# Turning token tiles and p by DMA instead of TensorE, ahead of attention and of the per-layer embedding

## The chip, the cores and the metric

The kernel runs on one core of one Trainium2 chip. The metric is the device time of one execution in microseconds; the kernel before takes 1997.2 us (median of 3 runs, 1996.89 to 1997.23).

## The reference

Two layers of a block are computed for 512 tokens of width 1024, in float32. A layer has four parts, each followed by a residual and a layer norm: a gated FFN (width 2816), a token mixer (stick-breaking attention, a chunked gated delta rule and a short convolution, called attention here), a second FFN, and the per-layer embedding.

```python
def reference(x, p, ln_g, ln_b, ffn_w_in, ...):
    for i in range(DEPTH):                                     # DEPTH = 2
        x = layer_norm(ALPHA * x + 0.5 * swiglu(x, ffn_w_in[i, 0], ffn_w_out[i, 0]), ln_g[i, 0], ln_b[i, 0])
        mix = token_mix(x, mix_w_in[i], ..., mix_w_out[i])
        x = layer_norm(ALPHA * x + mix, ln_g[i, 1], ln_b[i, 1])
        x = layer_norm(ALPHA * x + 0.5 * swiglu(x, ffn_w_in[i, 1], ffn_w_out[i, 1]), ln_g[i, 2], ln_b[i, 2])
        ple = jax.nn.sigmoid(x @ ple_w_gate[i] + ple_b_gate[i]) * (p[i] @ ple_w_proj[i])
        x = layer_norm(ALPHA * x + ple, ln_g[i, 3], ln_b[i, 3])
    return x
```

x is 512 x 1024, p is 512 x 256 for each layer, `ple_w_gate` 1024 x 1024, `ple_w_proj` 256 x 1024.

## The kernel before

The 512 tokens are four tiles (t = 0 to 3) of 128 tokens, the partitions of a core. x lies in SBUF twice: `x_tok`, tokens on the partitions, in float32, for residuals and norms; and `xT`, features on the partitions, for the matrix products, as two float16 parts, hi and lo, with lo the remainder after hi. Every product is three float16 matmuls (`mm3`, L278, L281, L282: hi by hi, hi by lo, lo by hi).

Weights come from memory in float32 by SyncE's DMA queue into one of three `raw` buffers (`load_rows`, 1 MB each). `split_part` makes the two halves: ScalarE copies raw, scaled, to hi (L141), VectorE subtracts (L142); a weight buffer has two such splits of 128x1024. A raw buffer is free for the next load when VectorE has made the second split from it.

The stages of a layer run one after the other: FFN, attention, FFN, embedding. An FFN works in four groups of hidden rows; at the end of each, `out_proj` multiplies the group's activations, up to four buffers `hT` of 4 KB a partition, by the output weights, tile by tile into the bank `po` (36 matmuls a tile in the last group), and VectorE adds to `x_tok` (L525). In the last group `norm_tile` follows each tile: statistics (L185, L187, L189), and four operations over 128x512 (L193, L197). `layer_norm` then puts the tile on the list `pending`.

`flush` turns what is pending: `to_T` does eight 128x128 float32 transposes on TensorE (L232) into two PSUM banks; ScalarE copies each bank to hi (L237), VectorE subtracts to lo (L238). It is called one tile later, so that TensorE has the next tile's products to do while the norm runs; the fourth tile's comes in the following stage.

The embedding (`ple`) loads four gate weights and the projection, one ring (`w1`) of five buffers of 8 KB beside a small pool for the bias `bg`, the norm constants and `pT`. For each tile it does the gate product (`pgate`, 48 matmuls), the projection of p (`pp`), sigmoid, product, residual and norm. p is loaded as `pr` and turned by 16 transposes on TensorE after the first tile's gate (L572), with L576 and L577 as its copies to hi and lo.

No order between the engines is written out: the tile framework's scheduler sets each engine's order when the program is built, by priorities and by its own cost model, and adds semaphore waits where a buffer or a value needs them. Pools that close give their space to the next ones, so the buffers of one stage lie where those of the stage before lay, and the first writes there wait for their last readers. Where the order on one engine is fixed by hand, `self.after(later, earlier)` ties two instructions without a semaphore. SyncE issues almost all transfers, in the order of its queue; an instruction there that waits holds all behind it.

The lines that the change touches, with what calls them, are these.

## Time and profile before

| | |
|---|---|
| median of 3 runs | 1997.2 us (1996.89 to 1997.23) |
| the profiled execution | 1997.55 us, span 1995.8 us, granted clock 0.998 |
| TensorE busy | 1950.1 us, 98% of the span |
| VectorE busy | 1522.4 us, 76% |
| ScalarE busy | 868.8 us, 44% |
| transposes of x on TensorE (L232) | 256, 36.1 us busy |
| transposes of p on TensorE (L572) | 16, 2.4 us busy |

Busy times of TensorE are sums of single durations that overlap in its pipeline; how long a batch holds the engine is read from the starts in order of time. In such rows the first number is the start in us from the span's beginning, the second the busy time of the merged rows, then engine, line, operation, output and inputs, and in brackets the idle time before it and what ended it. Stage by stage, the first layer's first FFN ends at 341.1 us, its second at 944.1 us.

### The profile page before, as it was taken

How to read it: one execution, taken by the hardware profiler on the slowest of the kernel's cores; microseconds unless marked ns; L12 is line 12 of the kernel's file. 1: busy time of each engine (PE TensorE's matmuls, PEld its weight loads, DVE VectorE, ACT ScalarE, POOL GpSimd, SP SyncE). 2: the span in 40 equal slices, each digit the busy share in tenths (PEclk: the TensorE clock that was granted, in tenths of full speed). 3: DMA queues.
4: the chain of work that ended last, by engine and by line, in shares of the span. 5: the costliest groups of instructions: out<-in, count | busy, mean ns of one | idle time of the engine just before them, and what ended most of it. 6: DMA issues, size and time to landing. Idle time of an engine off the chain costs nothing.

```text
span 1995.8 us, 33106 instructions
## 1 busy us (share of the span) xinstructions
PE 1950.1 (98%) x14058; PEld 1273.0 (64%) x14058; DVE 1522.4 (76%) x2347; ACT 868.8 (44%) x1294; POOL 69.9 (4%) x92
## 2 busy tenths in 40 slices
PE   7999999999999999999999999999999999999998
PEld 6677686545546677686467685854455466776853
DVE  8996866775679895859897877577756897967586
ACT  6454352454335453444264453424643364443431
POOL 1000000100000000000000000002000000000000
PEclk9999999999999999999999999999999999999999
DMA  8543320422162433334224343212222534333221
GB/s 239 184 126 103 89 86 1 130 56 64 65 196 79 148 106 106 106 120 146 94 85 127 106 124 88 65 55 78 53 86 82 173 96 138 106 106 85 96 74 43
DMA packets 245359, 205.15 MB, mean 103 GB/s; under 512 B 20846, under 2 KB 225500, under 8 KB 245212
## 3 DMA queue, kind: packets, MB, share of 16 engines
q1 hardware_dynamic: 245212, 203.05, 33.0%
q8 instruction: 110, 1.80, 0.4%
q14 instruction: 37, 0.30, 0.0%
HBM read 200.14 MB, written 2.88 MB: 102 GB/s over the span
## 4 chain that ended last, share of the span: by engine, by line
PE 73%; DVE 17%; ACT 6%; issue 2%; DMA 1%; POOL 0%; SPq 0%; DVEq 0%; ACTq 0%
PE po L282 7%; PE po L278 7%; PE po L281 7%; PE pA L278 6%; PE pA L281 6%; PE pA L282 6%; DVE wq L142 4%; DVE w L142 3%; PE pB L282 3%; PE pB L281 3%; PE pB L278 3%; ACT wq L141 2%; DVE f L492 1%; PE pC L281 1%; PE pC L282 1%
## 5 line engine op out<-in xcount | busy, mean ns | idle before, releaser
L142 DVE SCALAR_TENSOR_TENSOR wq<-f,wq 128x1024 f16<-128x1024 f32 (+1 forms) x240 | 335.2, 1399 | 18.4 <-ACT wq L141 15.3
L141 ACT ACTIVATE wq<-f 128x1024 f16<-128x1024 f32 (+1 forms) x240 | 279.4, 1191 | 126.5 <-PE pB L282 84.4
L141 ACT ACTIVATE w<-raw 128x1024 f16<-128x1024 f32 (+1 forms) x196 | 192.6, 1030 | 257.1 <-PE po L282 224.0
L278 PE MATMUL pA<-xS,wq 128*128 128x256 f16 x960 | 261.5, 272 | 7.9 <-ACT sg L447 3.9
L278 PE MATMUL po<-w,hT 128*128 128x512 f16 x704 | 266.9, 379 | 1.9 <-ACT hT L310 1.3
L282 PE MATMUL po<-w,hT 128*128 128x512 f16 x704 | 264.8, 379 | 2.7 <-DVE hT L311 2.7
L281 PE MATMUL po<-w,hT 128*128 128x512 f16 x704 | 266.8, 379 | 0.0
L282 PE MATMUL pA<-xS,wq 128*128 128x256 f16 x960 | 261.6, 273 | 0.0
L281 PE MATMUL pA<-xS,wq 128*128 128x256 f16 x960 | 261.6, 272 | 0.0
L142 DVE SCALAR_TENSOR_TENSOR w<-raw,w 128x1024 f16<-128x1024 f32 (+1 forms) x196 | 229.7, 1197 | 33.0 <-ACT w L141 33.0
L281 PEld LDWEIGHTS <-wq 128*128 128x128 f16 x2240 | 219.1, 98 | 44.8 <-issue 14.4
L492 DVE TENSOR_TENSOR f<-f 128x512 f32<-128x512 f32 x320 | 220.2, 690 | 27.2 <-DMA f<-in_ffn_w_in 22.1
L278 PEld LDWEIGHTS <-wq 128*128 128x128 f16 x2240 | 219.1, 98 | 29.9
L282 PEld LDWEIGHTS <-wq 128*128 128x128 f16 x2240 | 219.1, 98 | 27.1
L525 DVE SCALAR_TENSOR_TENSOR x_tok<-po,x_tok 128x512 f32<-128x512 f32 x144 | 97.5, 687 | 82.9 <-PE po L282 82.9
L282 PEld LDWEIGHTS <-hT 128*128 128x128 f16 x704 | 68.0, 98 | 86.2 <-DVE hT L311 6.5
L428 DVE TENSOR_TENSOR sg<-pB,sg 128x256 f32<-128x256 f32 x80 | 33.9, 423 | 115.6 <-PE pB L282 115.6
L278 PEld LDWEIGHTS <-hT 128*128 128x128 f16 x704 | 68.9, 98 | 79.7 <-ACT hT L310 3.4
L447 ACT ACTIVATE sg<-pA 128x256 f32<-128x256 f32 x80 | 30.6, 383 | 203.6 <-PE pA L282 203.6
L281 PEld LDWEIGHTS <-hT 128*128 128x128 f16 x704 | 68.9, 98 | 77.3 <-issue 1.5
L281 PEld LDWEIGHTS <-w 128*128 128x128 f16 x640 | 62.5, 98 | 61.3 <-issue 13.4
L282 PEld LDWEIGHTS <-w 128*128 128x128 f16 x640 | 62.5, 98 | 60.3 <-issue 5.4
(290 smaller groups left out, 3825.2 us busy)
## 6 DMA issues: line engine op xcount, KB each, us to landing
f<-in_ffn_w_in SPq DMA_DIRECT2D x160, 512.0 KB, 5.0
raw<-in_ffn_w_out SPq DMA_DIRECT2D x44, 1024.0 KB, 5.6
raw<-in_mix_w_in SPq DMA_DIRECT2D x28, 1024.0 KB, 5.5
raw<-in_mix_w_out SPq DMA_DIRECT2D x8, 1024.0 KB, 4.8
raw<-in_ple_w_gate SPq DMA_DIRECT2D x8, 1024.0 KB, 5.9
raw<-in_ffn_w_in SPq DMA_DIRECT2D x6, 1024.0 KB, 5.8
ln_gb<-in_ln_g SPq DMA_DIRECT2D x8, 512.0 KB, 3.9
ln_gb<-in_ln_b SPq DMA_DIRECT2D x8, 512.0 KB, 4.8
```

The source lines that it names most:

```text
L141: self.nc.scalar.activation(hi, raw, AF.Copy, scale=WS),
L142: self.nc.vector.scalar_tensor_tensor(lo, raw, WS, hi, op0=ALU.mult, op1=ALU.subtract),
L278: begun = nc.tensor.matmul(ps, a[0], b[0], start=first, stop=False, **k)
L281: nc.tensor.matmul(ps, a[0], b[1], start=False, stop=False, **k)
L282: return nc.tensor.matmul(ps, a[1], b[0], start=False, stop=last, **k)
L428: nc.vector.tensor_tensor(half(old.sg, 1), old.B, half(old.sg, 1), op=ALU.add)
L447: nc.scalar.activation(half(u.sg, 1), u.A, AF.Copy)
L492: total = nc.vector.tensor_tensor(f[:, to], f[:, a], f[:, b], op=ALU.add)
L525: self.nc.vector.scalar_tensor_tensor(xs, po[h], scale, xs, op0=ALU.mult, op1=ALU.add)
```

## The change

Attention and the embedding now get most of their turned tiles by transposing DMA. `pair_T` copies a tile in float16 into one buffer `turn` (ScalarE, 128x1024) and the remainder into a second (VectorE), and SyncE issues two `dma_start_transpose`, hi and lo, straight into `xT`. `turn`, called at the end of `layer_norm`, chooses by what stage follows: ahead of attention, tiles 0 to 2 are turned by DMA at once and tile 3 stays on TensorE by way of `pending`; ahead of an FFN all stay on TensorE; ahead of the embedding all four are kept on the list `turns` and done in `ple`: tiles 0 to 2 in SyncE's queue behind the projection's load, then bias and norm constants, then tile 3. p is loaded and turned the same way in the last group of the FFN before (`load_early`), as are the rows of constants for attention loaded; they have pools of their own, `tmp4` and `early`. The embedding's pool no longer holds `pT`.

```diff
@@ -41,12 +42,15 @@
         self.rawp = pool("rawp", bufs=3)
         self.w2 = pool("w2", bufs=4)
         self.tmp = pool("tmp", bufs=6)
+        self.tmp4 = pool("tmp4", bufs=2)
+        self.early = pool("early", bufs=1)
         self.small = pool("small", bufs=4)
         self.dram = pool("dram", bufs=2, space=bass.MemoryType.DRAM)
         self.psa = pool("psa", bufs=2, space=PSUM)
         self.psb = pool("psb", bufs=3, space=PSUM)
         self.psc = pool("psc", bufs=3, space=PSUM)
         self.pending, self.block_sums, self.put, self.behind = [], [], 0, None
+        self.turns = []
         self.constants()
 
     def bank(self, name, shape=(P, 512)):
@@ -171,9 +175,10 @@
         gb = pool.tile([P, 2, D], F32, name="ln_gb", tag=tag or "ln_gb", **k)
         g, b = gb[:, 0], gb[:, 1]
         dma = self.nc.sync.dma_start(g, self.ins["ln_g"][i, j : j + 1, :].to_broadcast([P, D]))
-        self.nc.sync.dma_start(b, self.ins["ln_b"][i, j : j + 1, :].to_broadcast([P, D]))
+        self.consts = self.nc.sync.dma_start(b, self.ins["ln_b"][i, j : j + 1, :].to_broadcast([P, D]))
         if after is not None:
             self.after(dma, after)
+            self.after(self.consts, after)
         return g, b
 
     def layer_norm(self, t, y, gb, last=False):
@@ -202,7 +207,7 @@
                     self.out[t * P : (t + 1) * P, h * 512 : (h + 1) * 512], yh
                 )
         if not last:
-            self.pending.append((self.xT, t, y, self.next_sums))
+            self.turn(self.xT, t, y)
 
     def norm_tile(self, t, gb, last):
 
@@ -259,6 +264,58 @@
             held.append(step)
         else:
             step()
+
+    def pair_T(self, out, pieces, wide=False):
+
+
+        nc = self.nc
+        hi, lo = (self.t2("turn", (P, D), F16) for _ in range(2))
+        if wide:
+            pieces, n = [pieces], D
+        else:
+            n = 512
+        for c, y in enumerate(pieces):
+            h, l = (v[:, c * n : (c + 1) * n] for v in (hi, lo))
+            if len(y.shape) == 3:
+                h, l = (v.rearrange("p (a b) -> p a b", b=y.shape[2]) for v in (h, l))
+            nc.scalar.activation(h, y, AF.Copy)
+            nc.vector.tensor_tensor(l, y, h, op=ALU.subtract)
+        return [nc.sync.dma_start_transpose(out(q), v) for q, v in enumerate((hi, lo))]
+
+    def turn(self, xT, t, y):
+
+
+        kind = self.following[2]
+        if kind == "p" and kind in KINDS:
+            self.turns.append((xT, t, y))
+        elif kind not in KINDS or t == NT - 1:
+            self.pending.append((xT, t, y, kind not in KINDS and kind == "f"))
+        else:
+            self.turn_now(xT, t, y)
+
+    def turn_now(self, xT, t, y, behind=None):
+        dmas = self.pair_T(lambda q: xT[:, q, :, t * P : (t + 1) * P], y, wide=True)
+        for dma in dmas if behind is not None else []:
+            self.after(dma, behind)
+        return dmas[1]
+
+    def load_early(self):
+
+        nc, ins = self.nc, self.ins
+        i, j, kind = self.following
+        if kind == "m":
+            rows = self.rows = self.early.tile([55, P], F32, name="rows", tag="rows")
+            nc.sync.dma_start(rows[0:48], ins["gdn_conv_w"][i].rearrange("t (c p) -> (t c) p", p=P))
+            nc.sync.dma_start(rows[48:54], ins["sc_conv_w"][i].rearrange("t (c p) -> (t c) p", p=P))
+            nc.sync.dma_start(rows[54:55], ins["gdn_norm_w"][i : i + 1, :])
+        if kind == "p":
+            pr = self.tmp4.tile([P, NT, 256], F32, name="pr", tag="ts")
+            nc.sync.dma_start(pr, ins["p"][i, 0].rearrange("(t p) e -> p t e", p=P))
+            pT = self.pT = self.tmp4.tile([P, 2, 2, S], F16, name="pT", tag="ts")
+            self.pair_T(
+                lambda q: pT[:, q].rearrange("p c (t k) -> p (c t) k", k=P),
+                [pr[:, :, c * P : (c + 1) * P] for c in range(2)],
+            )
 
     def put_sums(self, xS):
 
@@ -457,6 +514,8 @@
                 wo = weights((m1 - m0) // 2)
                 if gi == len(groups) - 1:
                     gb = self.ln_consts(i, j, self.w2, tag="w")
+                    if not last:
+                        self.load_early()
                 for t in range(NT):
                     self.out_proj(
                         t, lambda q, m: hT[(m0 + m) // 2][:, q, m % 2], wo, m1 - m0,
@@ -530,17 +589,17 @@
         self.xT = self.act.tile([P, 2, KD, S], F16, name="xT", tag="xT", bufs=2)
         with self.tc.tile_pool(name="ple", bufs=1, reuse_waits="tile") as pool, \
                 self.tc.tile_pool(name="w1", bufs=5, reuse_waits="tile") as self.w1:
-            pr = [self.t2("pr", (P, 2, 256)) for _ in range(2)]
-            for h in range(2):
-                nc.sync.dma_start(
-                    pr[h], ins["p"][i, 0, 256 * h : 256 * h + 256].rearrange("(t p) e -> p t e", p=P)
-                )
             wg = [self.load_rows(ins["ple_w_gate"][i], k, self.w1) for k in range(0, KD, 2)]
             wp = self.load_rows(ins["ple_w_proj"][i], 0, self.w1)
+
+            for args in self.turns[:-1]:
+                dma = self.turn_now(*args, behind=self.loaded)
             bg = pool.tile([P, D], F32, name="bg")
-            self.after(nc.sync.dma_start(bg, ins["ple_b_gate"][i : i + 1, :].to_broadcast([P, D])), self.loaded)
-            gb = self.ln_consts(i, j, pool)
-            pT = pool.tile([P, 2, 2, S], F16, name="pT")
+            self.after(nc.sync.dma_start(bg, ins["ple_b_gate"][i : i + 1, :].to_broadcast([P, D])), dma)
+            gb = self.ln_consts(i, j, pool, after=dma)
+            self.turn_now(*self.turns[-1], behind=self.consts)
+            self.turns = []
+            pT = self.pT
 
             def gift(t, h, behind=None):
                 pp = self.bank2("pp")
@@ -565,19 +624,6 @@
                         )
                     if last and t == NT - 1:
                         pps[h], done = gift(t, h, end)
-                if t == 0:
-                    for c in range(2):
-                        ps = self.bank2("ps_p", (P, NT, P))
-                        for tt in range(NT):
-                            nc.tensor.transpose(
-                                ps[:, tt], pr[tt // 2][:, tt % 2, c * P : (c + 1) * P], self.ident
-                            )
-                        hi = pT[:, 0, c].rearrange("p (t q) -> p t q", t=NT)
-                        nc.scalar.activation(hi, ps, AF.Copy)
-                        nc.vector.tensor_tensor(
-                            pT[:, 1, c].rearrange("p (t q) -> p t q", t=NT), ps, hi,
-                            op=ALU.subtract,
-                        )
                 self.flush()
                 for h in range(2):
                     hs = slice(h * 512, (h + 1) * 512)
@@ -629,10 +675,7 @@
         OFF_Q, OFF_K, OFF_V, OFF_Z, OFF_AB, OFF_SC = 768, 1280, 1792, 2304, 2816, 2824
 
-        rows = self.t2("rows", (55, P))
-        nc.sync.dma_start(rows[0:48], ins["gdn_conv_w"][i].rearrange("t (c p) -> (t c) p", p=P))
-        nc.sync.dma_start(rows[48:54], ins["sc_conv_w"][i].rearrange("t (c p) -> (t c) p", p=P))
-        nc.sync.dma_start(rows[54:55], ins["gdn_norm_w"][i : i + 1, :])
+        rows = self.rows
         hd = sm.tile([P, 2, 2], F32, name="hd", bufs=1)
         for e in range(2):
             for n, name in enumerate(("gdn_a_log", "gdn_dt_bias")):
@@ -1215,7 +1258,7 @@
     k.load_x()
     for (i, j, s), following in zip(n, n[1:] + [None]):
         last = following is None
-        k.next_sums = not last and following[2] == "f"
+        k.following = following
         if s == "f":
             k.ffn(i, 0 if j == 0 else 1, j, last)
         elif s == "m":
```

ScalarE ahead of the first layer's embedding, before (w<-raw are the splits of gate and projection weights; hT<-sg the FFN's last activations; xT<-ps_t the copies of turned tiles):

```order
L141 ACTIVATE w<-raw 128x1024 [waits DMAHW7_49,PE_49]
L310 ACTIVATE hT<-sg 128x512 [waits DVE_49,Activation_49]
L141 ACTIVATE w<-raw 128x1024
L141 ACTIVATE w<-raw 128x1024 [waits DMAHW0_49]
L141 ACTIVATE w<-raw 128x1024
L141 ACTIVATE w<-raw 128x1024 [waits DMAHW1_49]
L141 ACTIVATE w<-raw 128x1024
L141 ACTIVATE w<-raw 128x1024 [waits DMAHW2_49]
L141 ACTIVATE w<-raw 128x1024
L237 ACTIVATE xT<-ps_t 128x4x128 [waits PE_49] x4
L141 ACTIVATE w<-raw 128x1024 [waits DMAHW3_49,PE_49]
L141 ACTIVATE w<-raw 128x1024
```

The same place after (line numbers are those of the changed kernel: L145 is the split, L281 the copies to be turned, L367 the activations):

```order
L281 ACTIVATE turn<-x_tok 128x1024 [waits DVE_49]
L281 ACTIVATE turn<-x_tok 128x1024 [waits DMAHW1_49,DVE_49]
L281 ACTIVATE turn<-x_tok 128x1024 [waits DVE_49]
L145 ACTIVATE w<-raw 128x1024 [waits PE_49]
L145 ACTIVATE w<-raw 128x1024 x3
L145 ACTIVATE w<-raw 128x1024 [waits DMAHW2_49]
L145 ACTIVATE w<-raw 128x1024
L145 ACTIVATE w<-raw 128x1024 [waits DMAHW4_49]
L145 ACTIVATE w<-raw 128x1024
L145 ACTIVATE w<-raw 128x1024 [waits DMAHW5_49]
L145 ACTIVATE w<-raw 128x1024
L281 ACTIVATE turn<-x_tok 128x1024 [waits DMAHW6_49,DVE_49,Activation_49]
```

All splits of the gate's weights now stand behind the copies of tiles 0 to 2, and the first of them waits for TensorE. In the built program that wait is for the sixth matmul from the end of the FFN's last output product. The first gate buffer begins at byte 151424 of a partition, and so does the last of the four `hT` buffers, which that matmul reads; before, the embedding's pool held 4 KB more below the ring.

SyncE's queue at the embedding, before (raw are weights, bg and ln_gb the constants):

```order
L535 DMA pr<-in_p 128x2x256 [waits DMAHW7_49,DVE_49]
L535 DMA pr<-in_p 128x2x256 [waits DMAHW0_49,DVE_49]
L161 DMA raw<-in_ple_w_gate 128x2x1024 [waits DVE_49]
L161 DMA raw<-in_ple_w_proj 128x2x1024 [waits DVE_49]
L150 DMA raw<-in_ffn_w_in 128x8x256 [waits DMAHW3_49,DVE_49]
L150 DMA raw<-in_ffn_w_in 128x8x256 [waits DMAHW1_49,DMAHW4_49,DVE_49,Activation_49]
L161 DMA raw<-in_ffn_w_out 128x2x1024 [waits DMAHW2_49,DMAHW5_49,DVE_49,Activation_49]
L541 DMA bg<-in_ple_b_gate 128x1024 [waits DMAHW6_49,PE_49]
L173 DMA ln_gb<-in_ln_g 128x1024 [waits DMAHW7_49,PE_49]
L174 DMA ln_gb<-in_ln_b 128x1024 [waits DMAHW0_49]
```

And after:

```order
L165 DMA raw<-in_ple_w_proj 128x2x1024 [waits DMAHW5_49,DVE_49]
L283 DMA_TRANSPOSE xT<-turn 128x8x128 [waits DMAHW6_49,PE_49]
L283 DMA_TRANSPOSE xT<-turn 128x8x128 [waits DMAHW7_49]
L283 DMA_TRANSPOSE xT<-turn 128x8x128 [waits DMAHW0_49]
L283 DMA_TRANSPOSE xT<-turn 128x8x128 [waits DMAHW1_49]
L283 DMA_TRANSPOSE xT<-turn 128x8x128 [waits DMAHW2_49]
L283 DMA_TRANSPOSE xT<-turn 128x8x128 [waits DMAHW3_49]
L598 DMA bg<-in_ple_b_gate 128x1024 [waits DMAHW4_49,PE_49]
L177 DMA ln_gb<-in_ln_g 128x1024 [waits DMAHW5_49,PE_49]
L178 DMA ln_gb<-in_ln_b 128x1024 [waits DMAHW6_49]
L283 DMA_TRANSPOSE xT<-turn 128x8x128 [waits DMAHW7_49,Activation_49]
L283 DMA_TRANSPOSE xT<-turn 128x8x128 [waits DMAHW0_49,DVE_49]
```

The projection's load still waits for a split of VectorE's, as does the last gate load just ahead of it; six transposes now follow them, then the constants, and the last tile's two. The next FFN's weights, which stood between the projection and the bias, follow after all of these.

VectorE there, after (L584 residual, L190 to L202 norm of tile 3, L146 the splits):

```order
L584 SCALAR_TENSOR_TENSOR x_tok<-po,x_tok 128x512 [waits PE_49]
L190 BN_STATS st<-x_tok 128x6 [waits DVE_49]
L146 SCALAR_TENSOR_TENSOR w<-raw,w 128x1024 [waits Activation_49]
L192 BN_AGGR mv<-st 128x2 [waits DVE_49]
L146 SCALAR_TENSOR_TENSOR w<-raw,w 128x1024 [waits Activation_49]
L194 TENSOR_SCALAR rs<-mv 128x1 [waits DVE_49]
L198 SCALAR_TENSOR_TENSOR x_tok<-x_tok,mv,ln_gb 128x512 x2
L202 SCALAR_TENSOR_TENSOR x_tok<-x_tok,rs,ln_gb 128x512 [waits DVE_49,Pool_49]
L202 SCALAR_TENSOR_TENSOR x_tok<-x_tok,rs,ln_gb 128x512 [waits DVE_49]
L146 SCALAR_TENSOR_TENSOR w<-raw,w 128x1024 [waits DMAHW1_49,Activation_49]
L146 SCALAR_TENSOR_TENSOR w<-raw,w 128x1024 [waits Activation_49] x3
L146 SCALAR_TENSOR_TENSOR w<-raw,w 128x1024 [waits DMAHW4_49,Activation_49]
```

The splits of the first gate weight now stand inside the norm of the fourth tile, and the others behind it.

More of the change, by code (lines that the diff above doesn't have):

```diff
@@ L31 @@
 IWS = 1.0 / WS
+KINDS = "mp"
 class Block:
```

## The prediction

> **What bounds the kernel now.** I read the page's busy shares first, then the chain of waits, then the order in time of each engine around the two places where the change works: the end of the second FFN with the start of per-layer embedding, and the end of the first FFN with the start of attention.
>
> ```profile
> span 1995.8 us, 33106 instructions
> PE 1950.1 (98%) x14058; PEld 1273.0 (64%) x14058; DVE 1522.4 (76%) x2347; ACT 868.8 (44%) x1294; POOL 69.9 (4%) x92
> PE 73%; DVE 17%; ACT 6%; issue 2%; DMA 1%; POOL 0%; SPq 0%; DVEq 0%; ACTq 0%
> ```
>
> TensorE is busy 98% of the span. Whatever is taken off TensorE is a gain, and whatever makes it wait is a loss; the other engines count only through such waits. The profiled execution took 1997.55 us, 1.75 us more than its span and 0.35 us above the median of the runs shown (1997.2). I sum against 1997.55.
>
> At the boundary into per-layer embedding of the first layer, TensorE's rows in time are:
>
> ```profile
> 943.90 0.38 PE L282 MATMUL po<-w,hT 128*128 128x512 f16 x1
> 944.12 1.04 PE L232 MATMUL ps_t<-ident,x_tok 128*128 128x128 f32 x8
> 944.99 0.38 PE L278 MATMUL pgate<-w,xT 128*128 128x512 f16 x1
> ```
>
> There is no idle time: the last product of the FFN, eight transposes, the first product of the gate. Starts are 0.22 us apart for a product, and the batch of eight transposes holds the engine for 944.99 - 944.12 = 0.87 us. I call the end of the FFN's last output product s; here s = 944.12. That the gate can begin at once is due to ScalarE and the loads, which are far ahead:
>
> ```profile
> 908.83 1.05 ACT L141 ACTIVATE w<-raw 128x1024 f16<-128x1024 f32 x1
> 912.81 1.99 ACT L141 ACTIVATE w<-raw 128x1024 f16<-128x1024 f32 x2
> 915.22 2.93 ACT L141 ACTIVATE w<-raw 128x1024 f16<-128x1024 f32 x3
> 920.21 2.00 ACT L141 ACTIVATE w<-raw 128x1024 f16<-128x1024 f32 x2 [2.05 <-DMA raw<-in_ple_w_gate]
> 923.41 2.00 ACT L141 ACTIVATE w<-raw 128x1024 f16<-128x1024 f32 x2 [1.20 <-DMA raw<-in_ple_w_proj]
> ...
> 915.20 0.37 SPq L161 DMA_DIRECT2D raw<-in_ple_w_gate  x1
> 918.34 0.37 SPq L161 DMA_DIRECT2D raw<-in_ple_w_proj  x1
> ```
>
> The ten ScalarE halves of the splits (eight of the gate, two of the projection) start between 908.8 and 924.4, so 35 to 20 us before s. The last gate load goes out at 915.20 and releases its split at 920.21 (5.0 us); the projection's goes out at 918.34 and releases at 923.41 (5.1 us).
>
> **What the change removes.** These rows carry it:
>
> ```profile
> L232 PE MATMUL ps_t<-ident,x_tok 128*128 128x128 f32 x256 | 36.1, 287 | 7.6 <-DMA x_tok<-in_x 4.8 <-ACT ts L248 1.7 <-DVE x_tok L197 1.1
> L572 PE MATMUL ps_p<-ident,pr 128*128 128x128 f32 x16 | 2.4, 273 | 0.0
> ...
> 957.61 0.39 PE L278 MATMUL pp<-w,pT 128*128 128x512 f16 x1 [0.67 <-ACT pT L576]
> ```
>
> Of 256 transposes of x, 7 batches of eight go in each layer (three tiles before attention, four before the embedding): 14 x 0.87 = 12.2 us. The 16 transposes of p are two batches more, 1.7 us. The wait of 0.67 us for the turned p goes as well. **Gain: 14.6 us.** On VectorE and ScalarE a subtraction and a copy over 128x1024 replace two of each over 128x512, and neither engine sets TensorE's pace at these places, so I count nothing there. The early load of p and of the rows before attention stands ahead of other loads in SyncE's queue, in an FFN's last group, whose weights are by then on the way; nothing too.
>
> **What it adds at the embedding.** In the changed program, all ten ScalarE splits stand behind the three copies of tiles, and the first of them waits for TensorE. The layout explains the wait: p's turned tile, 4 KB a partition, has left the embedding's pool, so the weights' ring begins 4 KB lower, on the last of the FFN's four hT buffers. That buffer is read until the sixth matmul from the end of the last output product, 6 x 0.22 = 1.3 us before s. So the splits that were 20 to 35 us early now begin at s - 1.2. What follows goes by these rows (VectorE after the end of the first FFN, whose last product ends at 341.11, and one run of four splits):
>
> ```profile
> 341.11 1.04 PE L232 MATMUL ps_t<-ident,x_tok 128*128 128x128 f32 x8
> 341.99 0.28 PE L278 MATMUL pv<-wvab,xT 128*128 128x264 f16 x1
> 347.39 0.60 PE L232 MATMUL ps_t<-ident,x_tok 128*128 128x128 f32 x4
> ...
> 341.31 0.69 DVE L525 SCALAR_TENSOR_TENSOR x_tok<-po,x_tok 128x512 f32<-128x512 f32 x1 [1.75 <-PE po L282]
> 342.04 0.69 DVE L185 BATCH_NORM_STATS2 st<-x_tok 128x6 f32<-128x512 f32 x1
> 342.65 1.21 DVE L142 SCALAR_TENSOR_TENSOR w<-raw,w 128x1024 f16<-128x1024 f32 x1
> 344.51 1.41 DVE L193 SCALAR_TENSOR_TENSOR x_tok<-x_tok,mv,ln_gb 128x512 f32<-128x512 f32 x2
> 345.83 1.41 DVE L197 SCALAR_TENSOR_TENSOR x_tok<-x_tok,rs,ln_gb 128x512 f32<-128x512 f32 x2
> ...
> 952.44 4.63 DVE L142 SCALAR_TENSOR_TENSOR w<-raw,w 128x1024 f16<-128x1024 f32 x4
> ```
>
> VectorE's program order after s is: residual (from s + 0.2), statistics, first half of the gate's weight 0, aggregate, second half, four norm operations, then weights 1, 2 and 3. With 1.16 us a split and 1.32 us a pair of norm operations, weight 0 is whole at s + 4.0, the norm ends at s + 6.7, weight 1 is whole at s + 9.0, weight 2 at s + 11.35. There are three raw buffers. So the load of weight 3 waits for weight 0's split, goes out at s + 4.0, lands at s + 9.0, and its split ends at s + 13.65. The projection's load waits for weight 1's split, goes out at s + 9.0 and lands at s + 14.1. And **behind that load, in SyncE's queue, stand the six transposes of tiles 0 to 2**, with bias, norm constants and the last tile's two transposes behind them. TensorE's first gate product needs the high half of tile 0, its third the low half. Nothing is left on TensorE to cover this: the FFN is over.
>
> No transposing transfer runs in the kernel before, so I bound its price from both sides:
>
> ```profile
> TU<-dx SPq DMA_DIRECT2D x16, 32.0 KB, 2.3
> out<-x_tok SPq DMA_DIRECT2D x8, 256.0 KB, 2.0
> raw<-in_ple_w_proj SPq DMA_DIRECT2D x2, 1024.0 KB, 5.1
> raw<-in_ffn_w_in SPq DMA_DIRECT2D x4, 512.0 KB, 8.0
> DMA packets 7619, 5.65 MB, mean 283 GB/s; under 512 B 162, under 2 KB 7107, under 8 KB 7619
> ```
>
> From below: a transpose of 128x1024 f16 moves 256 KB, and the plain transfer of that size lands 2.0 us after its issue. If the transposes pass the load ahead of them, tile 0 is there at s + 9.4 + 2.0 = s + 11.4. Even with transposes that cost nothing, the gate's first half needs weight 3 for its last two of eight steps; split at s + 13.65, six steps of 0.65 us before it, so TensorE loses at least 13.65 - 3.9 = 9.7 us. From above: 5.1 us each, what a load four times as large takes. I take the streaming rate of the busiest stretch (the first 20 us), since the six stand in a full queue behind 1 MB: 0.262 MB / 283 GB/s = 0.93 us each, so tile 0's low half lands at 14.1 + 1.85 = s + 16.0. The transposes of tiles 1 and 2 and the bias (0.5 MB, 1.85 us) are in by about s + 21.5; the first buffers of the gate must be emptied by s + 16.0 + 48 x 0.216 = s + 26.4, so there is no second stall. **Loss: 16.0 us a layer.**
>
> A term for the restart: after an idle TensorE,
>
> ```profile
> 4.77 5.31 PE L232 MATMUL ps_t<-ident,x_tok 128*128 128x128 f32 x24 [4.77 <-DMA x_tok<-in_x]
> ```
>
> the first 24 transposes took 5.31 us, where three batches at 0.87 take 2.6. That 2.7 us more is part waiting for tiles and part perhaps a slow start; between 0 and 2.7 I take 1.35 a layer.
>
> **At attention.** Three batches less (counted above) lie between the last output product and the value products, and the fourth tile keeps TensorE. Its eight transposes now come after 48 value products, 5.4 us (341.99 to 347.39), at s + 5.4, while its norm ends at 347.24 = s + 6.1 by the rows above, at best 0.6 earlier without the low half of tile 2 that stood in between. So a new wait of 0 to 0.7 us; I take 0.65 a layer. The transposes of tile 2 are issued about 0.8 us before s and are needed after these products and the fourth tile's batch, at about s + 6.3; up to some 3.5 us each they are hidden, above that not.
>
> **The sum:** 1997.55 - 14.6 + 2 x (16.0 + 1.35 + 0.65) = 1997.55 + 21.4 = **2019 us**.
>
> **What the pages say of the price.** The Trainium skill, "Advanced Engine Details and Errata", section X-Bar Transpose (TRN2), has transposing transfers as fast as regular ones, which gives the same sum as the streaming rate. Its page "VectorE: DVE Perf Modes", section The three transpose paths, gives the DMA path 1309 ns for one 128x128 block and its rules prefer TensorE where PSUM will do; eight blocks in a row would be an estimated 10.5 us for each transfer, and this speaks against the change (rival 2). No run here shows either yet.
>
> **The rivals.**
>
> 1. *The transposes do not queue behind the projection's load* (each transfer on its own engines). For: the transfers use 16 engines, and 2.0 us for 256 KB is measured. Against: the loads of the first 20 us do queue (512 KB landing 8.0 us after issue, above). The stall is 11.4 us a layer: 1997.55 - 14.6 + 22.8 = 2006, and 2002 if weight 3 alone decides.
>
> 2. *A transpose is slow and the eight go one by one.* At 3 us each: tile 0 at s + 20.1, the bias at about s + 34 against a need at s + 30.5, so 23.6 + 2.7 + 0.65 a layer, 2037. At 5.1 us: tile 0 at s + 24.3, the bias at s + 46.5 against s + 34.7, so a stall of 36 and with the restart and attention 38 a layer, 2059. For: nothing measured bounds it. Against: only that all transfers shown of 256 KB or less take about 2 us. The VectorE page's rule is this rival at its extreme: its 10.5 us would put the embedding's eight at over 84 us a layer and the time far above 2100.
>
> 3. *The other side: the wait on the hT buffer does not bite.* If the first split runs as early as before (908.8, s - 35), loads and transposes are all done before s, and only the gain is left: 1997.55 - 14.6 + 1.3 = 1984. It decides from the point where that buffer comes free some 17 us before s, two tiles of output product earlier. Against: the wait stands in the program on a matmul of the last tile.
>
> 4. *Nothing measurable:* gain and stall cancel, which wants a stall of 7.3 us a layer, below the 9.7 that the weights alone give.
>
> **How the numbers follow.** My forecast has 0.62, its own range 2010 to 2027. Rival 1 has 0.14, rival 2 has 0.18 (most of it near 3 us), rival 3 has 0.04, rival 4 has 0.02. The range runs from 2005, the lower bound of rival 1, to 2038, the 3 us case: it leaves out rivals 3 and 4 and the slower part of rival 2. A measurement of this kernel tells some 0.2% (4 us) from no change: faster 0.04, same 0.02, slower 0.94.
>
> **What would show it.** In the profile after: TensorE idle some 16 us ahead of the first gate product in each layer, released by a transposing transfer; the ten splits of ScalarE after s - 1.3 and not 20 us before it; SyncE's projection load issued after s and the six transposes behind it; L232's successor with 144 transposes of x and none of p. The step is wrong if the gate begins within 9 us of s, if the idle ends with a split or the bias, if the transposes land before the projection's weights, or if the wait before attention's fourth tile is above 1 us.

## The result and the profile after

The changed kernel takes 2025.3 us (median of 4 runs, 2023.8 to 2025.9) against 1997.2: a ratio of 1.014, 95% interval 1.0127 to 1.0152. It is slower, by 28 us where I forecast 22. The profiled execution took 2025.29 us. From its page:

```profile
span 2023.6 us, 32874 instructions
PE 1943.6 (96%) x13930; PEld 1260.0 (62%) x13930; DVE 1526.1 (75%) x2333; ACT 869.2 (43%) x1280; POOL 69.9 (3%) x92
```

and its table of TensorE's waits (what waited, for whom; total us, times, longest):

```profile
PE pgate L335 <- DMA xT<-turn: 30.6, 2, 15.5
...
PE pgate L335 <- DVE gate L631: 3.7, 2, 2.8
PE zb L963 <- ACT hl L955: 3.6, 2, 2.4
```

The first two rows do not exist before; the third has 2.2 us there, at most 1.3 at a time. The transposes went as counted: the group of L237 (L232 before) has 144 members, and p has none.

```profile
L237 PE MATMUL ps_t<-ident,x_tok 128*128 128x128 f32 x144 | 21.9, 300 | 8.1 <-DMA x_tok<-in_x 4.5 <-DVE x_tok L202 2.3 <-ACT ts L253 1.2
```

Where the time went, from the starts of the first product of each stage on TensorE, in the two profiled executions:

| stage (from its first product to that of the next) | before | after | difference |
|---|---|---|---|
| layer 1: first FFN | 330.7 | 327.6 | -3.1 |
| layer 1: attention, up to its output product | 224.8 | 227.8 | +2.9 |
| layer 1: second FFN, up to the gate | 328.2 | 340.9 | +12.6 |
| layer 1: embedding | 57.0 | 60.9 | +3.9 |
| layer 2: first FFN | 328.8 | 326.3 | -2.5 |
| layer 2: attention | 224.7 | 225.0 | +0.3 |
| layer 2: second FFN, up to the gate | 328.5 | 341.2 | +12.7 |
| layer 2: embedding, up to the last product | 53.0 | 54.1 | +1.1 |

The stretch from attention's output product to the second FFN's first product takes 50.0 us in both layers of both kernels and is left out. With 0.2 less at the start the rows make +27.7, the difference of the two profiled executions. In order of time, the changed kernel's rows at the first layer's embedding (TensorE, ScalarE, SyncE's queue, VectorE) are:

```profile
941.76 0.38 PE L339 MATMUL po<-w,hT 128*128 128x512 f16 x1
957.28 0.61 PE L335 MATMUL pgate<-w,xT 128*128 128x512 f16 x1 [15.14 <-DMA xT<-turn]
970.07 0.38 PE L335 MATMUL pp<-w,pT 128*128 128x512 f16 x1
...
940.88 5.79 ACT L145 ACTIVATE w<-raw 128x1024 f16<-128x1024 f32 x6 [0.89 <-PE po L339]
956.28 2.00 ACT L145 ACTIVATE w<-raw 128x1024 f16<-128x1024 f32 x2 [3.37 <-DMA raw<-in_ple_w_proj]
...
945.95 0.37 SPq L165 DMA_DIRECT2D raw<-in_ple_w_gate  x1
950.93 0.37 SPq L165 DMA_DIRECT2D raw<-in_ple_w_proj  x1
951.40 10.94 SPq L283 DMA_TRANSPOSE xT<-turn  x6
962.44 0.52 SPq L598 DMA_DIRECT2D bg<-in_ple_b_gate  x1
969.86 1.20 SPq L154 DMA_DIRECT2D raw<-in_ffn_w_in  x2
...
948.55 6.90 DVE L146 SCALAR_TENSOR_TENSOR w<-raw,w 128x1024 f16<-128x1024 f32 x6
967.47 0.69 DVE L631 SCALAR_TENSOR_TENSOR gate<-pgate,bg 128x512 f32<-128x512 f32 x1 [6.60 <-DMA bg<-in_ple_b_gate]
990.04 1.28 DVE L631 SCALAR_TENSOR_TENSOR gate<-pgate,bg 128x512 f32<-128x512 f32 x2
```

The last output product ends at s = 941.76 + 0.22 = 941.98. ScalarE's first split starts at s - 1.1, released by TensorE; the last gate load goes out at s + 4.0, the projection's at s + 8.95, and it releases its split at s + 14.3. Right behind that load in the queue come the six transposes, and the gate begins at s + 15.3. In the second layer it begins at s + 15.6.

### The profile page after: what moved, and what is told of

The parts are those of the page before. It is cut to its first block, busy times and chain, and to the rows that moved or that the text cites. A ratio compares the mean times of both kernels' runs of the same rounds, so it can differ in the third digit from the quotient of the medians.

```text
span 2023.6 us, 32874 instructions
## 1 busy us (share of the span) xinstructions
PE 1943.6 (96%) x13930; PEld 1260.0 (62%) x13930; DVE 1526.1 (75%) x2333; ACT 869.2 (43%) x1280; POOL 69.9 (3%) x92
## 4 chain that ended last, share of the span: by engine, by line
PE 39%; DVE 8%; ACT 3%; issue 1%; DMA 0%; POOL 0%; DVEq 0%; SPq 0%; ACTq 0%
PE po L339 4%; PE po L335 4%; PE po L338 4%; PE pA L335 3%; PE pA L338 3%; PE pA L339 3%; DVE wq L146 2%; PE pB L339 2%; PE pB L338 2%; PE pB L335 2%; DVE w L146 1%; PE pgate L335 1%; PE pgate L338 1%; PE pgate L339 1%; ACT wq L145 1%
## 5 line engine op out<-in xcount | busy, mean ns | idle before, releaser
L146 DVE SCALAR_TENSOR_TENSOR wq<-f,wq 128x1024 f16<-128x1024 f32 (+1 forms) x240 | 334.2, 1395 | 18.5 <-ACT wq L145 15.3
L145 ACT ACTIVATE wq<-f 128x1024 f16<-128x1024 f32 (+1 forms) x240 | 279.4, 1191 | 126.5 <-PE pB L339 84.4
L145 ACT ACTIVATE w<-raw 128x1024 f16<-128x1024 f32 (+1 forms) x196 | 192.3, 1030 | 257.0 <-PE po L339 212.0
L146 DVE SCALAR_TENSOR_TENSOR w<-raw,w 128x1024 f16<-128x1024 f32 (+1 forms) x196 | 228.9, 1194 | 43.4 <-ACT w L145 43.3
L338 PEld LDWEIGHTS <-wq 128*128 128x128 f16 x2240 | 219.1, 98 | 44.4 <-issue 14.3
L584 DVE SCALAR_TENSOR_TENSOR x_tok<-po,x_tok 128x512 f32<-128x512 f32 x144 | 97.6, 686 | 87.3 <-PE po L339 87.3
L338 PEld LDWEIGHTS <-w 128*128 128x128 f16 x640 | 62.6, 98 | 62.9 <-issue 15.1
```

What stands on the lines that cost most here:

```text
L145: self.nc.scalar.activation(hi, raw, AF.Copy, scale=WS),
L146: self.nc.vector.scalar_tensor_tensor(lo, raw, WS, hi, op0=ALU.mult, op1=ALU.subtract),
L338: nc.tensor.matmul(ps, a[0], b[1], start=False, stop=False, **k)
L584: self.nc.vector.scalar_tensor_tensor(xs, po[h], scale, xs, op0=ALU.mult, op1=ALU.add)
```

## The experiments

The theory: the gate's weight ring lies on a buffer that the FFN still reads, so all weights are late, and the transposes, queued behind the late loads, are late with them. Rivals: the transposing transfers are slow by themselves; or the ring's place does little and only the queue's order matters.

**The ring where it was (e1_pad).** A tile that nothing uses fills the 4 KB that p's turned tile left.

```diff
             pT = self.pT
+            pool.tile([P, 2, 2, S], F16, name="pad")
```

> The changed kernel with a tile of 4 KB a partition that nothing uses put into the embedding's pool, so that the gate's weight ring begins where it began in the kernel before. Theory (the weights' ring lies on the last hT buffer, and that makes the splits late): the splits run some 20 us or more before the end of the last output product again, the two stalls of 15 us and the slow clock behind them are gone, and the time is 1997.2 - 14.6 + 1.3 = 1984 us, or up to 1988 where attention gives some 3 us back as it does in the changed kernel. Rival (the transposing transfers themselves are what TensorE waits for): a stall of 5 us or more a layer stays, and the time is 1997 us or more.

Measured: 1986.6 us, ratio to the kernel before 0.995 (0.9931 to 0.9961). Its ScalarE, SyncE and TensorE rows:

```profile
914.12 2.93 ACT L145 ACTIVATE w<-raw 128x1024 f16<-128x1024 f32 x3
922.93 2.00 ACT L145 ACTIVATE w<-raw 128x1024 f16<-128x1024 f32 x2 [0.52 <-DMA raw<-in_ple_w_proj]
...
925.91 1.25 SPq L283 DMA_TRANSPOSE xT<-turn  x1
938.01 8.67 SPq L283 DMA_TRANSPOSE xT<-turn  x5
...
942.18 0.38 PE L339 MATMUL pp<-w,pT 128*128 128x512 f16 x1
942.55 0.38 PE L335 MATMUL pgate<-w,xT 128*128 128x512 f16 x1
```

ScalarE is done with the splits 17 us before the gate, the six transposes are all issued by 946.7, and the gate starts right behind other products, with no wait. 4 KB of padding are worth 39 us, and the transposing DMA itself is no obstacle: the rival falls. This version beats both kernels.

**The ring moved, with nothing else (e2_low).** The kernel before, with p's turned tile in a pool of its own.

```diff
+        self.ptp = pool("ptp", bufs=1)
...
-            pT = pool.tile([P, 2, 2, S], F16, name="pT")
+            pT = self.ptp.tile([P, 2, 2, S], F16, name="pT")
```

> The kernel before with p's turned tile moved to a pool of its own and nothing else changed: all transposes stay on TensorE, but the gate's ring begins 4 KB lower, on the last hT buffer. Theory (the place of the ring alone costs time): the splits begin about 1 us before the end of the last output product, the fourth gate weight is split some 13.7 us after it, TensorE loses 9 to 12 us a layer in several pieces, and the time is 2017 us (2013 to 2024). Rival (without transposing transfers in the queue there is no loss): 1997 us.

Measured: 2007.6 us, ratio 1.005 (1.0033 to 1.0067). The place of the ring costs time without any DMA transpose, so the rival that puts all on the queue falls; but 5 us a layer, not 9 to 12. Its TensorE rows show the loss in pieces, each ended by VectorE:

```profile
946.73 0.38 PE L282 MATMUL pgate<-w,xT 128*128 128x512 f16 x1 [0.67 <-DVE w L143]
949.54 1.29 PE L233 MATMUL ps_t<-ident,x_tok 128*128 128x128 f32 x8 [1.36 <-DVE x_tok L198]
951.85 0.38 PE L282 MATMUL pgate<-w,xT 128*128 128x512 f16 x1 [1.01 <-DVE w L143]
959.32 0.38 PE L282 MATMUL pgate<-w,xT 128*128 128x512 f16 x1 [0.66 <-DVE w L143]
994.18 0.38 PE L279 MATMUL pgate<-w,xT 128*128 128x512 f16 x1 [0.90 <-DVE gate L586]
```

My bound of 9.7 us had the gate's first half wait for the fourth weight with nothing else to do. Between these waits TensorE has the fourth tile's transposes, p's, and other products. The last row is a wait for VectorE's gate late in the embedding; it comes up again under e9_last_pe.

**The ring low, but the queue free (e8_free_low).** The changed kernel without the ties that fix SyncE's order.

```diff
-                dma = self.turn_now(*args, behind=self.loaded)
+                self.turn_now(*args)
             bg = pool.tile([P, D], F32, name="bg")
-            self.after(nc.sync.dma_start(bg, ...), dma)
-            gb = self.ln_consts(i, j, pool, after=dma)
-            self.turn_now(*self.turns[-1], behind=self.consts)
+            self.after(nc.sync.dma_start(bg, ...), self.loaded)
+            gb = self.ln_consts(i, j, pool)
+            self.turn_now(*self.turns[-1])
```

> The changed kernel without the fixed order of SyncE's queue and without the pad: in the order as built, the transposes of tiles 0 to 2 then stand ahead of the last gate load and of the projection's, so tile 0 is turned long before it is needed, while the gate's splits still wait for the last output product. Theory (late weights cost at least 9.7 us a layer by themselves, the queue's order the rest): 1997.5 - 14.6 + 2 x 9.7 to 2 x 12 plus 3 in attention, 2005 to 2011 us. Rival (the transposes are the whole stall): below 1990 us.

Measured: 1999.35 us, ratio 1.001 (1.0 to 1.0019), below what I expected and above the rival. Its rows (SyncE, VectorE, TensorE):

```profile
924.31 18.00 SPq L283 DMA_TRANSPOSE xT<-turn  x6
945.62 0.38 SPq L165 DMA_DIRECT2D raw<-in_ple_w_gate  x1
...
948.22 6.89 DVE L146 SCALAR_TENSOR_TENSOR w<-raw,w 128x1024 f16<-128x1024 f32 x6
...
942.59 0.38 PE L335 MATMUL pgate<-w,xT 128*128 128x512 f16 x1 [0.56 <-DVE x_tok L584]
944.44 0.38 PE L338 MATMUL pgate<-w,xT 128*128 128x512 f16 x1 [1.47 <-DVE w L146]
949.49 0.38 PE L338 MATMUL pgate<-w,xT 128*128 128x512 f16 x1 [2.30 <-DVE w L146]
```

The weights are exactly as late as in the changed kernel (six splits done at 955.1, s + 13.5), yet TensorE waits 4.3 us, not 15. The order built for it differs: while the weights come in, the two halves of the first gate take turns at each weight, whereas in the changed kernel the first half goes through all four weights before the second begins. With tile 0 there, TensorE has twice the work for each weight.

**The queue free with the ring where it was (e6_free).** Both edits, pad and free queue, together.

> The padded kernel without the fixed order of SyncE's queue: the transposes, bias and norm constants are tied to nothing and stand where the scheduler puts them. Theory (once the weights are early, the queue has room and its order decides nothing): within 2 us of the padded kernel's 1986.6 us. Rival (the fixed order is needed so that transposes and loads don't hinder each other): 1990 us or more.

Measured: 1985.9 us, ratio 0.994 (0.9928 to 0.9958). The order of the queue matters only when the weights are late. The medians in one table:

| | ring on the hT buffer | ring where it was |
|---|---|---|
| all turns on TensorE | 2007.6 | 1997.2 |
| turns by DMA, queue in the fixed order | 2025.3 | 1986.6 |
| turns by DMA, queue free | 1999.4 | 1985.9 |

Late weights alone cost 13.4 us (1999.35 - 1985.91), the fixed order alone 0.7, which is less than the runs of one kernel differ by, both together 39.4: the fixed order ties the transposes, of which tile 0's could go 17 us before s, to a load that waits for a late split. With late weights the free queue came with another order on TensorE too (e8_free_low), so what lies between 2025.3 and 1999.4 belongs to the two orders together; no run parts them.

**The transposes one place earlier (e4_ahead).** Behind the last gate load, ahead of the projection's.

```diff
+            for args in self.turns[:-1]:
+                dma = self.turn_now(*args, behind=self.loaded)
             wp = self.load_rows(ins["ple_w_proj"][i], 0, self.w1)
-
-            for args in self.turns[:-1]:
-                dma = self.turn_now(*args, behind=self.loaded)
+            self.after(self.loaded, dma)
```

> The changed kernel with the six transposes queued behind the last gate load and ahead of the projection's load. Theory (the place behind the projection's load costs about 5 us of each stall, the late weights the rest): the stall ahead of the gate falls from 15.3 to about 10 us a layer and the time to about 2015 us (2011 to 2019). Rival (the transposes take as long wherever they stand, or delay the fourth gate weight): the stall stays above 13 us and the time above 2020 us.

Measured: 2015.95 us, ratio 1.009 (1.0078 to 1.0109), as the theory had it. TensorE's table of waits has this row, 20.7 us in two waits of about 10.4, where the changed kernel has two of about 15.3:

```profile
PE pgate L335 <- DMA xT<-turn: 20.7, 2, 10.4
```

**The two parts apart (e3_m, e5_p_pad).** Ahead of attention alone, with the embedding of the kernel before; and ahead of the embedding alone, with the pad (`KINDS = "m"` and `KINDS = "p"`).

> The part of the change ahead of attention alone; the embedding is that of the kernel before, p and all its tiles turned on TensorE. Theory (attention gives part of the gain back, since its small transfers and VectorE's order set its pace there): the first FFN of each layer ends 2.6 us earlier, and 1 to 3 us of it are lost again within attention, 1994 to 1996 us. Rival (the loss in attention is only the wait of 0.5 us before the fourth tile): 1997.2 - 2 x (2.6 - 0.5) = 1993 us.

> The padded kernel without the part ahead of attention: only p and the tiles ahead of the embedding are turned by DMA, and the 4 KB pad keeps the gate's ring where it was before. Theory (the two parts are nearly additive, and the one ahead of attention keeps about 2.4 us of its 5): batches 8 x 0.87 + 1.7 + 0.7 = 9.4 us less than before, 1988 us (1986.5 to 1990). Rival (the part ahead of attention is worth nothing): the same time as the padded kernel with both, 1986.6 us.

Measured: 1995.2 us for the first, ratio 0.9991 (0.9981 to 1.0), single runs from 1993.8 to 1999.0; 1990.0 us for the second, ratio 0.9962 (0.9949 to 0.9975). Both lie within what the theories gave, the second at its upper end. The part ahead of attention is worth 2 to 3.5 us of the 5.2 that it takes off the FFNs, and its interval touches no change.

**TensorE kept busy through the stall (e7_warm).** 64 products whose result nobody reads, between the last output product and the first gate product.

```diff
+            warm, done0 = self.bank2("warm"), self.po_end
+            for n in range(64):
+                end0 = nc.tensor.matmul(warm, self.ntri, pT[:, 0, 0], start=n == 0, stop=n == 63)
+                self.after(end0, done0)
+                done0 = end0
```

> The changed kernel with 64 products of 128x512 that nothing reads, on TensorE between the FFN's last output product and the gate's first (64 x 0.216 = 13.8 us of the stall of 15.3). Theory (the gate's first 5 us run at half the granted clock because TensorE stood idle): TensorE keeps its full clock, each layer gets 2.4 us back, 2020.5 us. Rival (the slow clock, or what looks like it, comes from transfers and weights arriving together with the first products): 2025 us.

The granted clock answers what slowed the gate's start. First the changed kernel by stretches (length, then busy us of PE, PEld, DVE, ACT, POOL, then the clock granted to TensorE, DMA share, GB/s), then the same of this one:

```profile
957.30:962.10 4.80, 4.80 (x12) 1.51 (x13) 3.50 (x3) 1.93 (x3) 0.00 (x0) 0.50 1.28 175
962.10:967.10 5.00, 5.00 (x25) 2.25 (x24) 0.00 (x0) 0.00 (x0) 0.00 (x0) 0.99 0.95 240
```

```profile
959.50:964.50 5.00, 5.00 (x23) 2.18 (x24) 3.50 (x3) 1.95 (x3) 0.00 (x0) 1.00 1.07 203
...
959.50 0.39 PE L335 MATMUL pgate<-w,xT 128*128 128x512 f16 x1 [1.55 <-DMA xT<-turn]
969.92 0.38 PE L335 MATMUL pp<-w,pT 128*128 128x512 f16 x1
```

In the first layer the changed kernel's gate has half the clock for 4.8 us and takes 970.07 - 957.28 = 12.8 us to its end; with the dummies the clock is 1.00 and it takes 10.4, with the DMA engines busy as before (share 1.07). So there the idle time makes the slow clock, and not the transfers. In the second layer the dummies did not keep the clock: it falls to 0.50 for 3.4 us, 1.3 us after the gate's first product, and the gate takes 12.1 us (1966.39 to 1978.52) against 12.9:

```profile
1966.39 0.39 PE L335 MATMUL pgate<-w,xT 128*128 128x512 f16 x1 [2.06 <-DMA xT<-turn]
...
1967.70:1971.10 3.40, 3.40 (x10) 1.21 (x8) 2.31 (x3) 0.68 (x1) 0.00 (x0) 0.50 1.02 190
```

The time did not fall: 2025.4 us median, ratio 1.014 (1.0122 to 1.0156). The expected 2020.5 us did not come, for two reasons. In the first layer the 2.4 us won come ahead of other waits: the embedding takes 61.05 us from its first gate product to the next FFN, against 60.9 in the changed kernel, with a new wait of 1.98 us for the norm and the two for VectorE's gate still there (2.93 and 0.90). In the second layer, where no such wait follows, only 0.8 us were won, and the embedding is that much shorter, 53.35 against 54.1. The gates also begin 0.2 and 0.4 us later behind s. The profiled execution, 2030.33 us, is the longest of its four; what it has above the median lies in its two attentions, 1.7 and 3.1 us longer than the changed kernel's.

**The fourth tile back on TensorE (e9_last_pe).** What holds the first layer's embedding back after the stall?

```diff
-            self.turn_now(*self.turns[-1], behind=self.consts)
+            self.pending.append((*self.turns[-1], False))
```

> The changed kernel with the last tile ahead of the embedding turned on TensorE instead of by DMA, all else as changed, the pad not used. Theory (the two waits of 2.8 and 0.9 us for VectorE later in the first layer's embedding come from the next FFN's weights, whose loads stand behind the last tile's two transposes and whose splits stand ahead of tile 1's gate on VectorE): those loads go out some 5.8 us earlier, the two waits are gone or below 1 us in sum, two batches of 0.87 us are back, 2023 us. Rival (the late bias is what holds VectorE back): the waits stay within 1 us of 3.7.

Measured: 2025.6 us, ratio 1.014 (1.0123 to 1.0157). Of the two waits for VectorE's gate the longer fell from 2.83 to 0.60 us, and the other stayed at 0.90 (the last two rows):

```profile
985.30 1.38 PE L237 MATMUL ps_t<-ident,x_tok 128*128 128x128 f32 x8 [1.09 <-DVE x_tok L202]
991.17 0.38 PE L335 MATMUL pgate<-w,xT 128*128 128x512 f16 x1 [0.60 <-DVE gate L631]
1006.05 0.38 PE L335 MATMUL pgate<-w,xT 128*128 128x512 f16 x1 [0.90 <-DVE gate L631]
```

A new one of 1.09 us came in (the first row), and VectorE reaches tile 1's gate at 990.44, as late as before (990.04), although the next FFN's first loads go out 6.1 us earlier (963.77). Between the two theories this run is inconclusive. The changed kernel's second layer says more, since no FFN follows it:

```profile
1969.72 0.69 DVE L631 SCALAR_TENSOR_TENSOR gate<-pgate,bg 128x512 f32<-128x512 f32 x1 [5.51 <-DMA bg<-in_ple_b_gate]
1981.99 0.68 DVE L631 SCALAR_TENSOR_TENSOR gate<-pgate,bg 128x512 f32<-128x512 f32 x1
```

There the bias is as late (s + 24.8 against s + 25.5), and TensorE has no such wait at all. So the late bias alone is not the cause. e4_ahead bears this out in the first layer: there VectorE has the bias in time and takes the first tile's gate right behind a split (first row), and TensorE's wait is as long as ever (last row):

```profile
965.39 1.28 DVE L631 SCALAR_TENSOR_TENSOR gate<-pgate,bg 128x512 f32<-128x512 f32 x2
975.03 6.89 DVE L146 SCALAR_TENSOR_TENSOR w<-raw,w 128x1024 f16<-128x1024 f32 x6
...
985.44 0.38 PE L335 MATMUL pgate<-w,xT 128*128 128x512 f16 x1 [2.91 <-DVE gate L631]
```

The six splits in the second row are the next FFN's; they stand ahead of tile 1's gate on VectorE in the first layer, and the second layer has none. That makes them the likely cause of the longer wait, but no run moves them alone. The wait of 0.90 us is another matter: every kernel with late weights has it, e2_low too, where no tile is turned by DMA, and the kernel before, e1_pad, e5_p_pad and e6_free have none. That is as far as the runs go.

## Why the prediction was right and where it was wrong

**The main step held.** The splits begin at s - 1.1 (foretold s - 1.2), the projection's load goes out at s + 8.95 (s + 9.0) and lands by s + 14.3 (s + 14.1), tile 0 follows about 1 us behind it, and TensorE stands 15.1 and 15.5 us. I took 16.0 from s: the gate starts with the high half at s + 15.3 and s + 15.6, and the low half was there by the third product, so charging up to the low half was 0.7 and 0.4 us too much. That the weights' place is the root is shown by e1_pad, and that the place in the queue is a part of the rest by e4_ahead; what e8_free_low took off belongs to the queue and to TensorE's other order together.

**The gain** of TensorE's batches came about as counted: 3.1 and 2.5 us in the two first FFNs for 2.6 foretold. In the second FFNs two batches and three of p's eight transposes (they stand ahead of the first tile's gate, not all behind it) fall before s; up to s these became 1.8 and 2.1 us shorter.

**"Even with transposes that cost nothing ... TensorE loses at least 9.7 us" was wrong.** It assumed that the gate's first half needs all four weights before anything else is done. With a free queue another order was built, and the same late splits cost 4.3 us of waits. The bound holds for the order of the changed kernel only, so what I gave as rival 1's least, 2002 us, was not a true lower end; the 2005 at which my range began lay above even that.

**The restart was mis-sized.** I took 1.35 us a layer between 0 and 2.7; it measured 2.4. The Trainium skill, "TensorE: Matmul & The Clock Gate", section Part 1: The HAM clock gate, says that after a window of some 3.4 us without work TensorE gets half its clock until it has been busy as long again. The changed kernel's trace agrees in kind: 0.50 for 4.8 us after 15 us of idle time. But in e7_warm the clock stayed at 1.00 after 1.55 us of idle time and fell to 0.50 for 3.4 us after 2.06 us, so here less idle time than such a window was enough.

**"There is no second stall" was wrong.** I had the bias in by s + 21.5; VectorE gets it at s + 25.5, since the six transposes hold SyncE's queue for 10.9 us (951.40 to 962.34) where my streaming rate had 5.6 us. That is still ahead of the s + 26.4 by which I needed it, and the second layer shows no wait with the bias as late. The 3.7 us of waits for VectorE's gate follow in the first layer, ahead of the products of tiles 2 and 3: I looked only at when the first tile's gate must be emptied, and not at what else stands in VectorE's order. They are a row of the sum that was missing.

**At attention** the wait ahead of the fourth tile is 0.49 us in each layer, for 0.65 foretold:

```profile
344.76 1.32 PE L237 MATMUL ps_t<-ident,x_tok 128*128 128x128 f32 x8 [0.49 <-DVE x_tok L202]
```

But attention gave back 2.9 us in the first layer and 0.3 in the second; beyond the wait foretold I had nothing there. Matched product by product, 1.2 us of the 2.9 are lost up to the products that wait for `g` on VectorE, and most of the rest around 70 us into the stage. There TensorE waits 2.42 us for ScalarE's `hl` (row `zb` of the table of waits) where the kernel before waits 0.99, and for 3.4 us behind it the granted clock is 0.50 where it was 1.00:

```profile
409.20:412.60 3.40, 3.40 (x13) 1.59 (x13) 3.31 (x10) 3.01 (x4) 0.00 (x0) 0.50 0.00 0
```

In the second layer that wait is 1.21 us, 1.26 before, and little is lost. Ahead of it in the first layer stand eight small transfers, whose issue takes longer than in the kernel before (first row after, second before); that they cause the wait is not shown:

```profile
392.07 4.93 SPq L864 DMA_DIRECT2D dm<-E  x8
```

```profile
394.19 3.79 SPq L821 DMA_DIRECT2D dm<-E  x8
```

The stage took 229.5 us in the profiled execution of e7_warm against 227.8 in the changed kernel, though nothing was changed there, so part of this varies between executions. What sets it stays open.

The terms against the forecast: stalls -1.1, restart +2.2, waits for VectorE's gate +3.7, attention +1.9, batches in the first FFNs -0.4, together the 6.3 us between the sum of +21.4 and the profiled +27.7; what is smaller cancels. The range held although the waits for VectorE's gate and most of attention's loss had no term in it: it was wide enough for them, which is luck and not reasoning.

**The rivals.** Rival 1 does not occur: with the transposes behind a full load, tile 0 is not there until that load is (5.9 us after its issue, 951.40 to 957.28; e4_ahead shows it for the place before, too). Rival 2 falls: a transpose does land 3.3 us after its issue, about the 3 us of that rival, but one is issued every 1.3 us and they overlap, and in e1_pad no wait is left. So of the page "VectorE: DVE Perf Modes" (the Trainium skill, section The three transpose paths), the 1309 ns for one 128x128 block can't be multiplied by eight: the eight blocks of a tile half landed 3.1 to 4.1 us after issue. Rival 3 is what the change does once the ring is back in its place: 1986.6 us, for 1984 worked out.

## What to carry to other kernels

A buffer that moves out of a pool moves all that lies behind it, and a ring that then falls on a buffer in late use can cost more than the edit brings: look for the first writer's wait, not at the size of the pool. A fixed queue order puts every transfer behind the latest load in it, so tie transfers to what they need and not to what happens to be ready early today. And a bound from "this must wait for that" holds for one order of the work only, so before calling it a floor, see what else the engine could do meanwhile.

## What the runs showed of the hardware

The transposing transfer of 128x1024 float16 takes SyncE longer to issue than a plain one (1.3 us; the plain loads above 0.4), and lands later than the plain 256 KB at 2.0 us. In the first row are the durations of the issues in ns (least, median, greatest); the second has the six of the 32 transposes, p's included, whose landing the profile gives:

```profile
L283 SPq DMA_TRANSPOSE xT<-turn x28: 1232/1306/5725, 321.4 to 1968.2; - x28
...
DMA to landing us min/median/max: 3.1/3.3/4.1
```

Six in a row held the queue 10.9 us; 3.4 us of it went to the second, which was issued while the 1 MB load ahead had not landed. What stands behind them in the queue waits as long. The Trainium skill's page "Advanced Engine Details and Errata", section X-Bar Transpose (TRN2), has them as fast as regular transfers, which these landing times don't bear out for this size.

Filling a stall with useless products kept the clock at 1.00 in one layer, where 1.55 us of idle time were left, and not in the other, where 2.06 us were left. Where it did, other waits took up the 2.4 us: what a slow clock ahead of another wait costs is not its whole length.
